# The last 512 output channels of a backbone layer's output projection kept in their own order, with a second copy of the router rows

## The chip, the cores and the metric

The kernel runs on one core of a Trainium2 chip. The metric is the device time of one execution in microseconds (us), as the median of several runs. Beside it stands one execution that the hardware profiler recorded; all durations below come from that execution. The engines are PE (TensorE; PEld is its weight load, the load of the stationary operand), DVE (VectorE), ACT (ScalarE), POOL (GpSimd) and SP, which here only issues DMAs.

## The reference, cut to what matters

One layer of a hybrid diffusion backbone, 256 latent and 256 context tokens, 2048 channels, float32:

```
mod  = silu(c) @ w_mod + b_mod                 # six vectors of 2048: sh1 sc1 g1 sh2 sc2 g2
u    = modulate(rmsnorm(h, norm_mix_w)) @ w_in
mix  = concat(ssd_branch(u), short_conv_branch(u)) @ w_out       # (4096) @ (4096, 2048)
h    = h + g1 * mix                                              # latent tokens only
f    = rmsnorm(h) * norm_ffn_w * (1 + sc2) + sh2
aff  = softmax(f @ w_router)                   # 16 experts; each takes its 32 best tokens
h    = h + g2 * expert_choice_ffn(f, aff, w_gate, w_up, w_down)
out  = rmsnorm(h)
```

The change lies in the output projection (`@ w_out`) for channels 1536 to 2047 and in the router product `f @ w_router` for the same channels.

## The kernel before

Large products run as three float32r passes: a weight tile is split into `whi` (rounded) and `wlo` (the rest), an activation likewise, and hi·hi, hi·lo and lo·hi are accumulated. `split_tile` does this for every tile of 128x1024 weights: SP loads `raw` (512 KB, L95, three buffers), ACT casts it to `whi` (L100), DVE subtracts to `wlo` (L101); `whi` and `wlo` also have three buffers. Its callers are the input projection (L338, `gemm_part`) and the output projection. Beside each tile run two paced streams: rows of `w_mod` for the second half of the modulation vectors (`mod_rows`: POOL loads a 256 KB `mraw`, DVE adds it to `macc`, L405, some 1.05 rows per tile in the output projection), and early loads of the first expert's weights into buffers as they come free (`first_weights`, L744, on SP's queue).

The output projection makes three passes over the 32 rows of 128 of `w_out`. Passes one and two (channels 0 to 1535, L856) hold the activations still and stream 512 weight columns. Pass three (channels 1536 to 2047, from `C3`) produces its result transposed: the weights are the stationary operand, 128 columns at a time, and 256 activations stream past. It takes 16 tiles; each needs 2 rows x 3 products x 4 column groups = 24 matmuls, 384 in all (L914). Which 128 of the 512 columns a group takes is what `in_fours` decides: group `i` takes columns `i, i+4, i+8, ...`, a step of four floats (16 bytes). The same order holds for the router: `w_router` lies in `gwr` as (block b, partition p, i), so its row `4p + i` of block b meets group `i`.

After pass three DVE adds the residual into `hT3` (tile `oh`, L918), ACT squares it (L920), PE accumulates the router's logits (L922) and the sums of squares (L925) into `pl`, and eight transposes bring `hT3` back into `h` (L930, copied by ACT at L931). From `pl` follow the softmax (L938 to L949), the choice of tokens (L967 on) and the gather of the first expert's tokens (L1038). Each expert then reads 24 MB of weights.

The order on each engine is set by a list scheduler from the order of the code; `issue_after` moves a block behind an instruction, `at_tick` delays it by so many weight tiles.

Of the kernel before, what the change touches and what calls it, by code (L numbers as in the profile page):

```python
# [11 lines left out]
OP = mybir.AluOpType  # L12
# [20 lines left out]
def layer(ctx: ExitStack, tc: tile.TileContext, x, c, cx, c_ctx, w_mod, b_mod, norm_mix_w, w_in,  # L33
# [27 lines left out]
    def sbank(name="s"):  # L61
        return bank("s", 4, name)
# [18 lines left out]
    def at_tick(n, fn):  # L81
        seq[0] += 1
        due.append((tick[0] + n, seq[0], fn))
# [48 lines left out]
    rows(r1[112:128], c_ctx)  # L132
    rows(r3, b_mod[0])

    r4 = pp.tile([13, 512], F32, name="r4")
    nc.gpsimd.dma_start(r4[0:4], norm_ffn_w[0].rearrange("(k p) -> k p", p=512))
    nc.gpsimd.dma_start(r4[4:12], b_mod[0, 3 * D:5 * D].rearrange("(k p) -> k p", p=512))
    nc.gpsimd.dma_start(r4[12:13], b_mod[0, 3 * D - 512:3 * D].rearrange("(k p) -> k p", p=512))
    hcol = const.tile([64, 2], F32, name="hcol")
    drow = pp.tile([2, KT], F32, name="drow")  # L140

# [65 lines left out]
    col2 = const.tile([P, 112], F32, name="col2")  # L207
    nc.vector.tensor_copy(col2, pt[:, 0:112])
    scw = col2[:, 0:48].rearrange("p (t k) -> p t k", t=3)
    nmix, _, nssm, nsc = (col2[:, 48 + 16 * i:64 + 16 * i] for i in range(4))  # L210

    pcol = const.tile([P, 3 * KT + 4], F32, name="pcol")
    nffn = pcol[:, 0:KT]

    cw = col1[:, 0:72].rearrange("p (t k) -> p t k", t=3)
# [3 lines left out]
    def late_cols():  # L219
        pt = sbank("pt")  # L220
        for i in range(4):
            nc.tensor.transpose(pt[:, 13 * i:13 * i + 13], r4.rearrange("p (c i) -> p i c", i=4)[:, i], ident[0:13, 0:13])
        nc.vector.tensor_copy(pcol.rearrange("p (a i) -> p i a", i=4),
                              pt[:, 0:52].rearrange("p (i c) -> p i c", i=4))
# [162 lines left out]

    mods = const.tile([P, 4, KT], F32, name="mods")
    sh2, G, g1c, g2c = (mods[:, i] for i in range(4))

    def mod_rows():

        for j in range(4):
            for q in range(4):
                dst = mods[:, j, 4 * q:4 * q + 4]
                c0 = (3, 4, 2, 5)[j] * D + 512 * q
                acc = mp.tile([P, 512], F32, name="macc", tag="macc", bufs=1)
                for k in range(KT):
# [9 lines left out]
                pc = sbank("pc")  # L408
                av = acc.rearrange("p (c i) -> p i c", i=4)
                fours = j < 2 or (j == 2 and q == 3)  # L410
                for i in range(4):
                    src = av[:, i] if fours else acc[:, P * i:P * i + P]
                    nc.tensor.transpose(pc[:, P * i:P * i + P], src, ident)

                def fin(j=j, q=q, dst=dst, c0=c0, pc=pc, fours=fours):
                    o = KT * (1 + j) + (4 * q if j < 2 else 0)
                    bias = pcol[:, o:o + 4] if fours else bcol[:, c0 // P:c0 // P + 4]
                    nc.vector.tensor_reduce(dst, pc.rearrange("p (j k) -> p j k", j=4), axis=mybir.AxisListType.X,
                                            op=OP.add)
                    nc.vector.tensor_tensor(dst, dst, bias, op=OP.add)  # L420
                    if j == 1:
                        nc.vector.scalar_tensor_tensor(dst, dst, 1.0, nffn[:, 4 * q:4 * q + 4], op0=OP.add, op1=OP.mult)
                at_tick(2, fin)
                yield

    def counted(steps):
# [366 lines left out]

    gwr = rp.tile([P, KT, 32], F32, name="gwr")
    wr = gwr[:, :, 0:NE]
    shw = hp_.tile([P, NE], F32, name="shw")
    g1 = []

    def prepare():
# [9 lines left out]
        nc.gpsimd.memset(gwr, 0.0)  # L809
        for b in range(4):  # L810
            nc.sync.dma_start(wr[:, 4 * b:4 * b + 4], w_router.rearrange("(b p i) e -> p b i e", p=P, i=4)[:, b])
        psb = sbank("psb")
        for k in range(KT):
            nc.tensor.matmul(psb[0:1, 0:NE], sh2[:, k:k + 1], wr[:, k], start=(k == 0), stop=(k == KT - 1))
# [8 lines left out]


    passes = ((0, 1024), (1024, 512))
    C3 = D - 512
# [59 lines left out]
    for i in range(0, 4, 2):  # L886
        pt = sbank("pt")
        for ii in range(2):
            for t in range(2):
                o = L * ii + P * t  # L890
                nc.tensor.transpose(pt[:, o:o + P], in_fours(h[:, t, C3:D])[:, i + ii], ident)
        nc.scalar.copy(hT3[:, i:i + 2], pt.rearrange("p (a b) -> p a b", a=2))

    pqs = rp.tile([P, L], F32, name="pqs", tag="hT", bufs=1)
# [12 lines left out]
    for k0 in range(0, 2 * KT, 2):  # L907
        hi, lo = split_tile(w_out, k0, C3, 512, 2)
        end = k0 == 2 * KT - 2
        todo = [(i, x) for x in products(k0, 2, hi, lo) for i in range(4)]  # L910
        if end:
            todo.sort(key=lambda x: x[0])
        for i, (j, pi, yy, w) in todo:
            nc.tensor.matmul(ov[i], in_fours(w[:, j])[:, i], yy, start=(k0 + j == 0 and pi == 0 and i % 2 == 0),  # L914
                             stop=(end and j == 1 and pi == 2), skip_group_check=True)
    for i in range(4):
        k = C3 // P + i
# [1 line left out]
        sq = rp.tile([P, L], F32, name="sq3", tag="hT" if i % 2 else "htmp", bufs=1)  # L919
        nc.scalar.activation(sq, hT3[:, i], AF.Square)  # L920
        for t in range(2):
            nc.tensor.matmul(pl[:, NE * t:NE * t + NE], hT3[:, i, P * t:P * t + P], gwr[:, k, 0:NE], start=False,  # L922
                             stop=(i == 3), skip_group_check=True)
        for t in range(2):
            nc.tensor.matmul(pl[:, 2 * NE + t:2 * NE + t + 1], sq[:, P * t:P * t + P], ones[:, 0:1], start=False,  # L925
                             stop=(i == 3), skip_group_check=True)
    for t in range(2):
        pt = sbank("pt")
        for i in range(4):
            nc.tensor.transpose(pt[:, P * i:P * i + P], hT3[:, i, P * t:P * t + P], ident)  # L930
        nc.scalar.copy(in_fours(h[:, t, C3:D]), pt.rearrange("p (i c) -> p i c", i=4))  # L931

    mod_rows_to(16 * KT)
    flush()
# [264 lines left out]
```

## Time and profile before

| | us |
|---|---|
| median of three runs (2007.34 to 2010.8) | 2009.35 |
| the profiled execution's own time | 2005.08 |
| its span in the trace | 2003.2 |
| output projection, passes one and two | 797 to 958 |
| output projection, pass three | 958 to 1052 |
| router, choice of tokens, gather | 1052 to 1078 |
| experts | 1078 to the end |

To read the profile: a stage is the stretch between two times of the trace; in it one looks for the engine that is never idle and for the wait that ends last. A PE pace is taken from the starts of its matmuls, not from their durations, since matmuls overlap.

### The profile page before, as it was taken

The page shows a single profiled execution, that of the slowest core. Times are in us where ns is not written, and L with a number is a line of the kernel's source. Part 1 is how long each engine was busy: PE and PEld are TensorE (multiplying, and loading weights), DVE is VectorE, ACT ScalarE, POOL GpSimd, SP SyncE. Part 2 cuts the span into 40 slices and gives each one's busy share as a digit, 9 for nine tenths or more (in the row PEclk, how much of TensorE's full clock was granted, in tenths as well). Part 3 has the DMA queues.
Part 4 walks back from the last instruction along what each step waited for, and adds up shares of the span by engine and source line. Part 5 has one row for each costly group of instructions (what it writes and reads, how often), then busy time and mean ns, then how long its engine had stood idle before and what let it go on. Part 6 is the DMA issues. An engine that isn't in the chain of part 4 may idle for free.

```text
span 2003.2 us, 25499 instructions
## 1 busy us (share of the span) xinstructions
PE 1671.1 (83%) x10340; PEld 1047.1 (52%) x10340; DVE 900.9 (45%) x1387; ACT 515.9 (26%) x847; POOL 183.9 (9%) x314
## 2 busy tenths in 40 slices
PE   6999999999999999999998766766766676666675
PEld 5677997878788999777993111111111111111122
DVE  2457985778778789777422111111011111101113
ACT  4323555574674344434211000000000000000002
POOL 1000110212112232322100000000000000000000
PEclk9999999999999999999998888888788888878888
DMA  9964783546367998888638999999999999999996
GB/s 356 405 230 121 238 266 101 164 125 216 89 209 257 341 301 298 293 315 291 214 128 327 422 428 427 427 427 428 426 428 427 428 426 427 427 428 427 427 427 259
DMA packets 149270, 641.12 MB, mean 320 GB/s; under 512 B 16649, under 2 KB 35334, under 8 KB 125216
## 3 DMA queue, kind: packets, MB, share of 16 engines
q1 hardware_dynamic: 127984, 570.19, 73.5%
q0 software_dynamic: 20880, 68.25, 9.9%
q8 instruction: 81, 1.33, 0.3%
q10 hardware_dynamic: 288, 1.05, 0.1%
q14 instruction: 37, 0.30, 0.0%
HBM read 637.34 MB, written 2.10 MB: 319 GB/s over the span
## 4 chain that ended last, share of the span: by engine, by line
DMA 44%; PE 39%; issue 7%; DVE 5%; ACT 2%; SPq 1%; POOL 1%; DVEq 0%; ACTq 0%; POOLq 0%
DMA abig<-in_w_up_dram 15%; PE g L335 11%; PE g L338 10%; DMA ebig<-in_w_up_dram 7%; DMA mwt<-in_w_up_dram 5%; DMA mwt<-in_w_down_dram 5%; PE gu L1076 4%; DMA mraw<-in_w_mod_dram 3%; DMA raw<-in_w_in_dram 3%; DMA ebig<-in_w_down_dram 3%; PE g L856 2%; DMA abig<-in_w_down_dram 2%; PE g L914 2%; PE yd L1109 2%; DVE wlo L101 2%
## 5 line engine op out<-in xcount | busy, mean ns | idle before, releaser
L338 PE MATMUL g<-abig,whi 128*128 128x256 f32 x2048 | 370.8, 285 | 4.9 <-ACT whi L100 2.8
L101 DVE TENSOR_TENSOR wlo<-raw,whi 128x1024 fp32r<-128x1024 f32 x241 | 295.7, 1230 | 168.2 <-ACT whi L100 167.0
L100 ACT CAST whi<-raw 128x1024 fp32r<-128x1024 f32 x241 | 254.0, 1055 | 381.9 <-DMA raw<-in_w_in_dram 87.2
L1076 PE MATMUL gu<-abig,xe 128*32 128x512 f32 x1200 | 247.0, 799 | 109.2 <-DMA abig<-in_w_up_dram 101.4
L338 PEld LDWEIGHTS g<-abig,whi 128*128 128x128 f32 x2048 | 316.8, 193 | 11.0 <-issue 5.4
L338 PE MATMUL g<-abig,wlo 128*128 128x256 f32 x1024 | 281.6, 286 | 1.7 <-DVE wlo L101 1.6
L1081 DVE SCALAR_TENSOR_TENSOR hid<-hid,gu 64x512 f32<-64x512 f32 x16 | 10.9, 679 | 496.4 <-ACT hid L1080 496.4
L335 PE MATMUL g<-abig,whi 128*128 128x512 f32 (+1 forms) x672 | 215.5, 399 | 3.7 <-ACT abig L319 2.0
L1076 PEld LDWEIGHTS gu<-abig,xe 128*32 128x32 f32 x1200 | 54.6, 139 | 274.6 <-DMA abig<-in_w_up_dram 133.7
L1080 ACT ACTIVATE hid<-gu 64x512 f32<-64x512 f32 x16 | 9.5, 591 | 729.1 <-PE gu L1076 729.1
L405 DVE SCALAR_TENSOR_TENSOR macc<-mraw,csl,macc 128x512 f32<-128x512 f32 x240 | 184.5, 769 | 26.4 <-DMA mraw<-in_w_mod_dram 23.8
L338 PEld LDWEIGHTS g<-abig,wlo 128*128 128x128 f32 x1024 | 192.8, 193 | 4.1 <-DVE wlo L101 3.2
L400 POOL DMA_DIRECT2D mraw<-in_w_mod_dram x256 | 138.2, 540 | 601.5 <-DVE macc L405 322.6
L1076 PE MATMUL gu<-ebig,xe 128*32 128x512 f32 x432 | 116.1, 812 | 53.7 <-DMA ebig<-in_w_up_dram 50.0
L1076 PE MATMUL gu<-mwt,xe 128*32 128x512 f32 x416 | 109.9, 791 | 41.4 <-DMA mwt<-in_w_up_dram 32.6
L335 PEld LDWEIGHTS g<-abig,whi 128*128 128x128 f32 (+1 forms) x672 | 122.4, 185 | 40.1 <-issue 8.8
L335 PE MATMUL g<-abig,wlo 128*128 128x512 f32 (+1 forms) x336 | 131.0, 394 | 0.0
L856 PE MATMUL g<-whi,abig 128*128 128x512 f32 x384 | 112.8, 397 | 4.7 <-ACT whi L100 4.6
L1123 DVE TENSOR_TENSOR m<-m,g 128x512 f32<-128x512 f32 x112 | 69.8, 682 | 62.9 <-PE g L1119 62.9
L1076 PEld LDWEIGHTS gu<-ebig,xe 128*32 128x32 f32 x432 | 24.2, 138 | 122.0 <-DMA ebig<-in_w_up_dram 64.3
L856 PEld LDWEIGHTS g<-whi,abig 128*128 128x128 f32 x384 | 72.4, 190 | 22.1 <-ACT whi L100 6.3
L1056 POOL DMA_DIRECT2D h<-in_final_norm_w_dram x1 | 0.6, 578 | 847.1 <-PE pt L1038 847.1
(339 smaller groups left out, 1855.4 us busy)
## 6 DMA issues: line engine op xcount, KB each, us to landing
raw<-in_w_in_dram SPq DMA_DIRECT2D x177, 512.0 KB, 4.6
abig<-in_w_gate_dram SPq DMA_DIRECT2D x35, 2048.0 KB, 38.7
abig<-in_w_up_dram SPq DMA_DIRECT2D x35, 2048.0 KB, 36.6
mraw<-in_w_mod_dram POOLq DMA_DIRECT2D x256, 256.0 KB, 4.5
abig<-in_w_down_dram SPq DMA_DIRECT2D x30, 2048.0 KB, 36.2
big<-in_w_mod_dram SPq DMA_DIRECT2D x32, 1024.0 KB, 10.8
raw<-in_w_out_dram SPq DMA_DIRECT2D x64, 512.0 KB, 5.2
mwt<-in_w_down_dram SPq DMA_DIRECT2D x16, 2048.0 KB, 34.8
```

Of the source, the lines that this page charges most:

```text
L100: nc.scalar.copy(hv, wv)
L101: sub = nc.vector.tensor_tensor(lv, wv, hv.bitcast(F32), op=OP.subtract)
L335: nc.tensor.matmul(banks[ct][0:ncol], st, a[q][:, kk], start=beg, stop=end)
L338: nc.tensor.matmul(banks[ct // 2][0:ncol, o:o + L], st, a[q][:, kk, L:2 * L], start=beg and ct % 2 == 0, stop=end, skip_group_check=True)
L400: nc.gpsimd.dma_start(w, w_mod[P * k:P * k + P, c0:c0 + 512])
L405: nc.vector.scalar_tensor_tensor(acc, w, cs, acc, op0=OP.mult, op1=OP.add)
L856: nc.tensor.matmul(ob[nn * t + m], yy[:, P * t:P * t + P], w[:, j, 512 * m:512 * m + 512], start=(k0 + j == order[0] and pi == 0), stop=(k ...
L914: nc.tensor.matmul(ov[i], in_fours(w[:, j])[:, i], yy, start=(k0 + j == 0 and pi == 0 and i % 2 == 0), stop=(end and j == 1 and pi == 2), ...
L1076: nc.tensor.matmul(gu[32 * q:32 * q + 32], xe[:, k], wt[q // 2][:, 1024 * kk + 512 * (q % 2):1024 * kk + 512 * (q % 2) + 512], start=(k == ...
L1081: nc.vector.scalar_tensor_tensor(hid, hid, 1.0, gu[0:64], op0=OP.add, op1=OP.mult)
L1109: nc.tensor.matmul(yd[32 * q:32 * q + 32], hidT[:, j, 32 * (c // 2):32 * (c // 2) + 32], parts[i][:, 512 * q:512 * q + 512], start=(c == 0 ...
L1123: nc.vector.tensor_tensor(av, h[:, t, 512 * q:512 * q + 512] if e_ == 0 else av, pc[q], op=OP.add)
```

## The change

The last 512 channels are no longer dealt out in fours. Each matmul of pass three takes 128 neighbouring columns as its stationary operand, and the two transposes of the residual ahead of it do the same. The router therefore needs its rows of these channels in their own order too: a tile `wr3` (128 x 4 x 16) is loaded a second time from `w_router`, in pieces of 16 floats, and multiplied by `G3`, a second copy of the factor norm_ffn_w * (1 + sc2) in that order. `G3` costs four more transposes and three small DVE instructions in `mod_rows` (one block of 512 columns is turned twice). The bias of `g1` for these channels comes from `bcol` now, so a 2 KB load at the start falls away. The eight transposes back into `h` are written behind the last sum of squares, and ACT's copy writes 512 neighbouring floats.

```diff
-    nc.gpsimd.dma_start(r4[12:13], b_mod[0, 3 * D - 512:3 * D].rearrange("(k p) -> k p", p=512))
...
+    G3 = const.tile([P, 4], F32, name="G3")
...
+                def columns(dst, fours, bias, norm):
+                    pc = sbank("pc")
+                    for i in range(4):
+                        src = av[:, i] if fours else acc[:, P * i:P * i + P]
+                        nc.tensor.transpose(pc[:, P * i:P * i + P], src, ident)
...
+                if j < 2:
+                    o = KT * (1 + j) + 4 * q
+                    columns(dst, True, pcol[:, o:o + 4], nffn[:, four] if j == 1 else None)
+                else:
+                    columns(dst, False, bias, None)
+                if j == 1 and q == 3:
+                    columns(G3, False, bias, nffn_[:, four])
...
+    wr3 = rp.tile([P, 4, NE], F32, name="wr3")
...
+        nc.sync.dma_start(wr3, w_router[C3:D].rearrange("(b p) e -> p b e", p=P))
+        nc.vector.tensor_tensor(wr3, wr3, G3.rearrange("p (k o) -> p k o", o=1).to_broadcast([P, 4, NE]), op=OP.mult)
...
-                nc.tensor.transpose(pt[:, o:o + P], in_fours(h[:, t, C3:D])[:, i + ii], ident)
+                nc.tensor.transpose(pt[:, o:o + P], h[:, t, C3 + P * (i + ii):C3 + P * (i + ii + 1)], ident)
...
-            nc.tensor.matmul(ov[i], in_fours(w[:, j])[:, i], yy, start=(k0 + j == 0 and pi == 0 and i % 2 == 0),
+            nc.tensor.matmul(ov[i], w[:, j, P * i:P * i + P], yy, start=(k0 + j == 0 and pi == 0 and i % 2 == 0),
...
-            nc.tensor.matmul(pl[:, NE * t:NE * t + NE], hT3[:, i, P * t:P * t + P], gwr[:, k, 0:NE], start=False,
+            nc.tensor.matmul(pl[:, NE * t:NE * t + NE], hT3[:, i, P * t:P * t + P], wr3[:, i], start=False,
...
-    for t in range(2):
-        pt = sbank("pt")
-        for i in range(4):
-            nc.tensor.transpose(pt[:, P * i:P * i + P], hT3[:, i, P * t:P * t + P], ident)
-        nc.scalar.copy(in_fours(h[:, t, C3:D]), pt.rearrange("p (i c) -> p i c", i=4))
+    with tc.issue_after(done.ins):
+        for t in range(2):
+            pt = sbank("pt")
+            for i in range(4):
+                nc.tensor.transpose(pt[:, P * i:P * i + P], hT3[:, i, P * t:P * t + P], ident)
+            nc.scalar.copy(h[:, t, C3:D], pt)
```

Within pass three the matmuls stand in the same order as before. At two places the instructions stand differently.

PE, before, at the end of pass three (L922 is the router's product, L925 the sums of squares, L930 the transposes back into `h`, L950 the turn of the softmax):

```order
L914 MATMUL g<-abig,whi 128x256
L922 MATMUL pl<-gwr,oh 128x16 x2
L930 MATMUL pt<-ident,oh 128x128 x4
L925 MATMUL pl<-ones,sq_10009 128x1 x2
L922 MATMUL pl<-gwr,oh 128x16 x2
L925 MATMUL pl<-ones,sq_10016 128x1 x2
L922 MATMUL pl<-gwr,oh 128x16 x2
L930 MATMUL pt<-ident,oh 128x128 x4
L925 MATMUL pl<-ones,sq_10023 128x1 x2
L922 MATMUL pl<-gwr,oh 128x16 x2
L925 MATMUL pl<-ones,sq_10030 128x1 x2
L950 MATMUL pa<-ident,aff 16x128 x2
```

PE, after, at the same place (the lines have moved by eleven or twelve):

```order
L925 MATMUL g<-abig,whi 128x256
L933 MATMUL pl<-wr_8224,oh 128x16 x2
L936 MATMUL pl<-ones,sq_10020 128x1 x2
L933 MATMUL pl<-wr_8224,oh 128x16 x2
L936 MATMUL pl<-ones,sq_10027 128x1 x2
L933 MATMUL pl<-wr_8224,oh 128x16 x2
L936 MATMUL pl<-ones,sq_10034 128x1 x2
L933 MATMUL pl<-wr_8224,oh 128x16 x2
L936 MATMUL pl<-ones,sq_10041 128x1 x2
L942 MATMUL pt<-ident,oh 128x128 x8
L962 MATMUL pa<-ident,aff 16x128 x2
```

The eight transposes stand behind the last sum of squares now, between it and the turn of the softmax.

SP, after, in pass one, where the router's rows are loaded (before, the three `gwr` loads stood behind twelve `raw` loads of `w_out`, with no `wr` load):

```order
L95 DMA raw<-in_w_out_dram 128x1024 x11
L822 DMA wr_8224<-in_w_router_dram 128x4x16
L95 DMA raw<-in_w_out_dram 128x1024
L821 DMA gwr<-in_w_router_dram 128x4x16 x3
L95 DMA raw<-in_w_out_dram 128x1024
```

The new load stands between the eleventh and the twelfth tile of `w_out`.

DVE, after, at the same place (the first `wlo` here is that of the ninth tile of `w_out`; `wr_8224` is `wr3`, `G_1528` is `G3`):

```order
L101 TENSOR_TENSOR wlo<-raw,whi 128x1024
L405 SCALAR_TENSOR_TENSOR macc<-mraw,csl,macc 128x512 x2
L101 TENSOR_TENSOR wlo<-raw,whi 128x1024
L823 TENSOR_TENSOR wr_8224<-wr_8224,G_1528 128x64
L101 TENSOR_TENSOR wlo<-raw,whi 128x1024
```

The product with `G3` stands between the tenth and the eleventh tile's subtraction; it is the first reader of the new load.

## Rows read from the trace of the kernel before

**Rows 1.** The page: PE's granted clock and the DMA engines' share, 40 slices.

```profile
PEclk9999999999999999999998888888788888878888
DMA  9964783546367998888638999999999999999996
```

**Rows 2.** Stretches: length, busy time (instructions) of PE, PEld, DVE, ACT, POOL; clock, DMA, GB/s.

```profile
690.00:740.00 50.00, 50.00 (x420) 50.00 (x419) 44.18 (x57) 22.00 (x25) 19.17 (x27) 1.00 0.90 298
740.00:790.00 50.00, 49.13 (x411) 48.93 (x410) 45.23 (x58) 23.03 (x27) 16.29 (x29) 1.00 0.96 326
850.00:900.00 50.00, 44.24 (x183) 34.51 (x184) 38.08 (x46) 17.14 (x19) 11.01 (x21) 0.97 0.89 318
957.80:1051.50 93.70, 93.70 (x416) 92.62 (x415) 29.46 (x38) 19.56 (x25) 4.31 (x8) 1.00 0.49 163
```

**Rows 3.** Groups in pass three: busy us, mean ns | idle before, releaser.

```profile
L101 DVE TENSOR_TENSOR wlo<-raw,whi 128x1024 fp32r<-128x1024 f32 x15 | 18.4, 1225 | 52.0 <-ACT whi L100 52.0
L100 ACT CAST whi<-raw 128x1024 fp32r<-128x1024 f32 x14 | 14.7, 1049 | 45.4 <-PE g L914 43.7 <-PE g L856 1.7
```

**Rows 4.** Lines L914 and L338: duration ns min/median/max; first and last start.

```profile
L914 PEld LDWEIGHTS g<-abig,whi x256: 307/330/334, 957.8 to 1051.6; 128*128 128x128 f32 x128
L338 PEld LDWEIGHTS g<-abig,whi x2048: 186/192/333, 199.5 to 799.9; 128*128 128x128 f32 x187
```

**Rows 5.** PE in order of time, in pass three and in the input projection.

```profile
997.41 2.03 PE L914 MATMUL g<-abig,whi 128*128 128x256 f32 x8
999.28 1.09 PE L914 MATMUL g<-abig,wlo 128*128 128x256 f32 x4
1000.21 2.03 PE L914 MATMUL g<-abig,whi 128*128 128x256 f32 x8
...
702.35 0.64 PE L338 MATMUL g<-abig,whi 128*128 128x256 f32 x4
702.83 0.28 PE L338 MATMUL g<-abig,wlo 128*128 128x256 f32 x1
```

**Rows 6.** Weight loads of line L413 in two blocks, columns in fours, then neighbouring.

```profile
L413 PEld LDWEIGHTS pc<-ident,macc x4: 198/204/210, 828.1 to 828.5; 128*128 128x128 f32 x4
...
L413 PEld LDWEIGHTS pc<-ident,macc x4: 138/140/142, 878.5 to 878.9; 128*128 128x128 f32 x4
```

**Rows 7.** All engines in order of time from pass three's end to the first expert.

```profile
1052.18 1.94 SPq L744 DMA_DIRECT2D abig<-in_w_gate_dram  x4
1052.35 0.63 PE L930 MATMUL pt<-ident,oh 128*128 128x128 f32 x4
1052.82 0.50 PE L925 MATMUL pl<-ones,sq 128*128 128x1 f32 x4
...
1054.52 0.63 PE L930 MATMUL pt<-ident,oh 128*128 128x128 f32 x4
...
1056.43 0.16 DVE L938 SCALAR_TENSOR_TENSOR rh<-pl,rh 128x2 f32<-128x2 f32 x1 [3.37 <-PE pl L925]
...
1071.71 3.81 PE L1038 MATMUL pt<-h,oh 128*32 128x512 f32 x16
...
1078.10 0.62 PE L1076 MATMUL gu<-ebig,xe 128*32 128x512 f32 x2 [1.18 <-DVE xe L1051]
```

**Rows 8.** DMA issues: KB each, median us from issue to landing.

```profile
raw<-in_w_out_dram SPq DMA_DIRECT2D x64, 512.0 KB, 5.2
ebig<-in_w_gate_dram SPq DMA_DIRECT2D x8, 512.0 KB, 9.2
gwr<-in_w_router_dram SPq DMA_DIRECT2D x4, 32.0 KB, 5.7
drow<-in_ssm_d_dram POOLq DMA_DIRECT2D x1, 0.1 KB, 7.2
```

**Rows 9.** DVE in pass one: subtractions of the eighth and the tenth tile of `w_out`.

```profile
819.04 1.23 DVE L101 TENSOR_TENSOR wlo<-raw,whi 128x1024 fp32r<-128x1024 f32 x1 [1.62 <-ACT whi L100]
...
825.07 1.21 DVE L101 TENSOR_TENSOR wlo<-raw,whi 128x1024 fp32r<-128x1024 f32 x1
```

More of the change, by code (lines that the diff above doesn't have):

```diff
@@ L133, in layer @@
     rows(r3, b_mod[0])
-    r4 = pp.tile([13, 512], F32, name="r4")
+    r4 = pp.tile([12, 512], F32, name="r4")
     nc.gpsimd.dma_start(r4[0:4], norm_ffn_w[0].rearrange("(k p) -> k p", p=512))
     nc.gpsimd.dma_start(r4[4:12], b_mod[0, 3 * D:5 * D].rearrange("(k p) -> k p", p=512))
-    nc.gpsimd.dma_start(r4[12:13], b_mod[0, 3 * D - 512:3 * D].rearrange("(k p) -> k p", p=512))
     hcol = const.tile([64, 2], F32, name="hcol")
@@ L209, in layer @@
     scw = col2[:, 0:48].rearrange("p (t k) -> p t k", t=3)
-    nmix, _, nssm, nsc = (col2[:, 48 + 16 * i:64 + 16 * i] for i in range(4))
-    pcol = const.tile([P, 3 * KT + 4], F32, name="pcol")
+    nmix, nffn_, nssm, nsc = (col2[:, 48 + 16 * i:64 + 16 * i] for i in range(4))
+    pcol = const.tile([P, 3 * KT], F32, name="pcol")
     nffn = pcol[:, 0:KT]
@@ L221, in late_cols @@
         for i in range(4):
-            nc.tensor.transpose(pt[:, 13 * i:13 * i + 13], r4.rearrange("p (c i) -> p i c", i=4)[:, i], ident[0:13, 0:13])
+            nc.tensor.transpose(pt[:, 12 * i:12 * i + 12], r4.rearrange("p (c i) -> p i c", i=4)[:, i], ident[0:12, 0:12])
         nc.vector.tensor_copy(pcol.rearrange("p (a i) -> p i a", i=4),
-                              pt[:, 0:52].rearrange("p (i c) -> p i c", i=4))
+                              pt[:, 0:48].rearrange("p (i c) -> p i c", i=4))
         nc.gpsimd.dma_start(hcol[:, 0:1], ssm_dt_bias.rearrange("o h -> h o"))
@@ L407, in mod_rows, with fin @@
                         yield
-                pc = sbank("pc")
                 av = acc.rearrange("p (c i) -> p i c", i=4)
-                fours = j < 2 or (j == 2 and q == 3)
-                for i in range(4):
[L412 to L423, printed above, removed]
+                def columns(dst, fours, bias, norm):
[3 more added lines that the diff above has]
+                        nc.tensor.transpose(pc[:, P * i:P * i + P], src, ident)
+                    def fin():
+                        nc.vector.tensor_reduce(dst, pc.rearrange("p (j k) -> p j k", j=4), axis=mybir.AxisListType.X,
+                                                op=OP.add)
+                        nc.vector.tensor_tensor(dst, dst, bias, op=OP.add)
+                        if norm is not None:
+                            nc.vector.scalar_tensor_tensor(dst, dst, 1.0, norm, op0=OP.add, op1=OP.mult)
+                    at_tick(2, fin)
+                four, bias = slice(4 * q, 4 * q + 4), bcol[:, c0 // P:c0 // P + 4]
+                if j < 2:
[5 more added lines that the diff above has]
+                    columns(G3, False, bias, nffn_[:, four])
                 yield
@@ L795, in layer @@
     wr = gwr[:, :, 0:NE]
+    C3 = D - 512
+    wr3 = rp.tile([P, 4, NE], F32, name="wr3")
     shw = hp_.tile([P, NE], F32, name="shw")
@@ L825, in layer @@
     passes = ((0, 1024), (1024, 512))
-    C3 = D - 512
     hs = const.tile([P, 2, 3], F32, name="hs")
@@ L921, in layer @@
         for t in range(2):
-            nc.tensor.matmul(pl[:, NE * t:NE * t + NE], hT3[:, i, P * t:P * t + P], gwr[:, k, 0:NE], start=False,
+            nc.tensor.matmul(pl[:, NE * t:NE * t + NE], hT3[:, i, P * t:P * t + P], wr3[:, i], start=False,
                              stop=(i == 3), skip_group_check=True)
         for t in range(2):
-            nc.tensor.matmul(pl[:, 2 * NE + t:2 * NE + t + 1], sq[:, P * t:P * t + P], ones[:, 0:1], start=False,
-                             stop=(i == 3), skip_group_check=True)
-    for t in range(2):
-        pt = sbank("pt")
-        for i in range(4):
-            nc.tensor.transpose(pt[:, P * i:P * i + P], hT3[:, i, P * t:P * t + P], ident)
-        nc.scalar.copy(in_fours(h[:, t, C3:D]), pt.rearrange("p (i c) -> p i c", i=4))
+            done = nc.tensor.matmul(pl[:, 2 * NE + t:2 * NE + t + 1], sq[:, P * t:P * t + P], ones[:, 0:1], start=False,
+                                    stop=(i == 3), skip_group_check=True)
+    with tc.issue_after(done.ins):
[4 more added lines that the diff above has]
+            nc.scalar.copy(h[:, t, C3:D], pt)
     mod_rows_to(16 * KT)
```

## The prediction, made before the changed kernel ran

> **What bounds the kernel now.** I read the slices first. The DMA engines are busy nine tenths or more from slice 22 on, that is through the experts, and there the granted clock is 0.8; slice 20, in pass three, has DMA at 3 tenths with the clock at 0.9 or more [rows 1]. So the experts are a DMA stage of fixed length, and whatever makes pass three end earlier moves them forward. Then the stretches: in pass three PE is busy 93.7 of 93.7 us at clock 1.00 (the 2.4 GHz level) while DMA stands at 0.49 and DVE and ACT at under a third [rows 2]. Next, who waits for whom there: ACT's cast waits 43.7 us for L914 to give back a `whi` buffer, and DVE waits 52.0 us for that cast [rows 3]. Nobody is late for PE. Pass three is a PE stage, and its pace is the question.
>
> The pace is odd. From 997.41 to 1000.21 PE starts 12 matmuls of L914, one each 233 ns; in the input projection four of L338 start in 0.48 us, one each 120 ns [rows 5]. Both have 128x128 float32r weights and 256 float32r activations as they stream, and the clock is 1.00 in both stretches [rows 2]. What differs in the operands is the step of the stationary one: neighbouring columns in L338, every fourth in L914. The weight load shows it: 330 ns in L914, 192 ns in L338 [rows 4]. A second pair settles most of the doubt: line L413 turns blocks of `macc` with the columns taken in fours for some blocks and in a row for others, and the same instruction loads its weights in 204 ns in the first case and in 140 ns in the second [rows 6].
>
> **The change part by part.** The sum goes from the profiled execution's own time, 2005.08 us (span 2003.2), which lies 4.3 us under the median of the runs, 2009.35; I take the same difference off the median.
>
> *Pass three's matmuls.* 384 matmuls go from 233 to 120 ns: 384 x 0.1133 = **43.5 us off** the path. The step is the same in all 384, the tile shape is that of L338, so I take L338's pace whole. Pass three would last some 93.7 - 43.5 = 50.2 us.
>
> *What is late next in pass three.* At the new pace a tile takes 2.88 us, as in the input projection, whose loads have the same size and whose `mod_rows` stream is no slower. There PE kept busy 50.00 and 49.13 of 50 us at 298 and 326 GB/s [rows 2]. Pass three moves 93.7 us x 163 GB/s = 15.3 MB; in 50.2 us that is 304 GB/s, between those two. The worst stretch at such a load is 850 to 900, where early loads stood between the `raw` loads: 44.24 of 50 busy at 318 GB/s [rows 2]. So the bounds are 0 and 12% of 50 = 6 us; I take 3%, **1.5 us on**, near the two stretches with the same matmuls, since in pass three the `raw` loads run ahead of most early loads. DMA time is no harder bound: 0.49 x 93.7 = 46 us of it fits in 50, at a share of 0.91, and 0.96 was reached [rows 2].
>
> *The end of pass three.* Four transposes stand between products and sums of squares twice. The next L925 starts 0.47 us after each L930 group begins [rows 7], and the second sum of squares frees the buffer that the next square needs. With both groups behind the last L925, DVE's L938 comes about 2 x 0.47 = **1 us** sooner. The transposes then fill the time in which PE waits for the softmax; the gather that reads `h` starts 15 us after L938 [rows 7], so they and ACT's copies cost nothing (without that cover some 2 us). Bounds 0 to 2.
>
> *The second copy.* G3 adds four transposes in the input projection, where PE is the bound: four at 0.12 us or a little more, **0.5 us on**. Its three DVE instructions lie in a stage where DVE is busy 44 to 45 of 50 us [rows 2]: about 1 us fits in the gaps; uncovered it would be that 1 us. The 2 KB load that goes, the contiguous transposes of the residual and the contiguous copy into `h` lie beside other work: nothing.
>
> *The load of `wr3`.* It is a wait in DVE's queue that was not there. SP issues it behind the eleventh `raw`, whose buffer is free when the eighth subtraction ends, at 820.3; DVE reaches the product behind the tenth, at 826.3 [rows 9]. That is 6.0 us of cover. Queued behind it on DVE stand the eleventh `wlo` and all `macc` work, and PE waits for that `wlo`; on SP the twelfth `raw` waits for the ninth subtraction anyway. The router's other loads, 128 pieces of 256 bytes each, land in 5.7 us; 32 pieces of 4 bytes (`drow`) in 7.2; half a megabyte queued among others in 9.2 [rows 8]. `wr3` has 512 pieces of 64 bytes, which no row shows. Near the first three the wait is 0 to 3.2 us, and PE has about a tile's subtraction of lead, 1.2 us. I take **1 us on**, bounds 0 and 3; the far bound is a rival below.
>
> Sum: -43.5 + 1.5 - 1.0 + 0.5 + 1.0 = -41.5 us. The profiled execution would take 1963.6 us, the median 2009.35 - 41.5 = 1967.9, so **1968 us**.
>
> *Behind pass three* nothing should give the gain back. The last four early loads start when pass three frees its last buffer, at 1052.18, and the first expert's matmuls at 1078.10, after the chain through the softmax [rows 7]. Both ends of that 26 us stretch hang on the end of pass three, so it moves as a piece, and the experts behind it read the same bytes.
>
> **The rivals.**
>
> *DMA becomes the bound of pass three* (the ring of three `raw` buffers runs dry). For it: pass three would ask 304 GB/s where it now asks 163, and in its second half half-megabyte early loads stand between the `raw` loads; such loads have taken 9.2 us to land [rows 8]. A buffer's round is landing, cast (1.05) and subtraction (1.23) [rows 3]: at 9.2 us, 11.5 / 3 = 3.8 us for a tile, 0.95 over the 2.88, for some 8 tiles 7.6 us; with the bound of 6 us for the rest of the pass 14 us at most. Against it: at 5.2 us [rows 8] a round gives 2.5 us for a tile, and buffers are ahead at the start, as ACT's waits show [rows 3]. It would give 1974 to 1982 us.
>
> *No gain in the pace.* L914 also goes round four accumulators, one matmul each, where L338 stays on one, and that might set 233 ns. Against it: the weight load itself is longer, and L413 differs by the step alone [rows 4, 6]. Then only the small terms are left, 0.5 + 1 - 1 us (without the faster pace nothing is late in pass three), about 2010 us. The Trainium skill has a rule that would come to this: "TensorE: Matmul & The Clock Gate", section "LDWEIGHTS (loading the stationary operand)", gives the time of a weight load as the number of columns over 1.2, 107 ns for 128, with nothing on their step. The trace disagrees with it by 330 against 192 ns at the same 128 columns, so it gets little of the chance.
>
> *Slower: the `wr3` load stalls DVE.* Place: DVE's queue between the tenth and the eleventh subtraction, 826.3. If time went by pieces, at `drow`'s 7.2 / 32 = 0.225 us each, 512 pieces would take 115 us; less 6 of cover and 1 of lead, 108 us on, and 2009 - 42.5 + 108 = 2075 us. It makes the kernel slower from a landing of about 7 + 42 = 50 us. Against it: 128 pieces land in 5.7 us, less than `drow`'s 32 [rows 8], so most of the 7.2 us is no time for pieces.
>
> **How the numbers follow.** Forecast 0.81, DMA-bound pass three 0.13, no gain 0.04, slower 0.02. The forecast's own range: the terms at their low ends give -43.5 - 2 + 0.5 = -45 us, 1964, less 2 to 4 us for the spread of the runs and for the lower profiled execution, 1960; at the high ends -43.5 + 6 + 0.5 + 3 = -34 us, 1975. To take in the greater part of the second case the range goes to 1979. Faster than before by over 0.2% (4 us, about what a measurement of this kernel can tell from no change): 0.81 + 0.13 = 0.94; within 0.2%: 0.04; slower: 0.02.
>
> **What would show it.** In the profile after: weight loads of pass three at about 192 ns and a start each 120 ns; pass three some 50 us long with PE busy over 95% and DMA at about 0.9; the first expert's matmuls some 42 us earlier; the experts' length unchanged; the first L936 straight behind the router's product; DVE's product for `wr3` with a wait of under 3 us in front. The prediction is wrong if the loads stay at 330 ns; if they fall but PE idles over 6 us in pass three; or if pass three ends 42 us earlier and the first expert doesn't.

## The result and the profile after

The changed kernel takes 1965.04 us, the median of four runs (1960.28 to 1965.16), against 2009.47 for four runs of the kernel before (2007.34 to 2010.8): a ratio of 0.9774, 95% interval 0.9757 to 0.9791, so 44.4 us less. The forecast was 1968, range 1960 to 1979. The profiled execution of after took 1965.03 us (span 1963.2), that of before 2005.08 (span 2003.2). Those two differ by 40.05 us, and the stages below are compared between them.

| stage | before | after | difference |
|---|---|---|---|
| start of the trace to pass three's first matmul | 958.01 | 958.65 | +0.64 |
| pass three, first matmul to first router product | 93.98 | 50.22 | -43.76 |
| first router product to first expert's first matmul | 26.11 | 26.70 | +0.59 |
| first expert's first matmul to the end of the span | 925.1 | 927.6 | +2.5 |
| sum (span) | 2003.2 | 1963.2 | -40.0 |

The page of after, granted clock and DMA share in 40 slices of 49 us (counted from 0, as in the prediction), answers to [rows 1]:

```profile
PEclk9999999999999999999989877878888889888787
DMA  9964784455465999899898999999999999999996
```

The dip to 3 tenths in slice 20 is gone: pass three now lies in slices 19 and 20, at 8 and 9 tenths. The stretches of pass three and of the time before it (length; busy time and instructions of PE, PEld, DVE, ACT, POOL; clock, DMA share, GB/s) answer to [rows 2]:

```profile
850.00:900.00 50.00, 46.26 (x201) 36.10 (x197) 39.37 (x48) 17.81 (x19) 11.82 (x22) 0.93 0.92 325
958.60:1008.90 50.30, 50.30 (x419) 49.17 (x418) 29.17 (x37) 18.97 (x25) 4.30 (x8) 1.00 0.85 302
```

Pass three is still a PE stage. PE is busy 50.30 of 50.30 us at clock 1.00 (the 2.4 GHz level), and DMA went from 0.49 to 0.85, 163 to 302 GB/s. The matmul line of pass three, now L925 (duration ns min/median/max, first and last start), and its pace in order of time answer to [rows 4] and [rows 5]:

```profile
L925 PEld LDWEIGHTS g<-abig,whi x256: 186/192/201, 958.4 to 1008.6; 128*128 128x128 f32 x128
...
L925 PE MATMUL g<-abig,whi x256: 278/283/384, 958.6 to 1008.8; 128*128 128x256 f32 x128
```

```profile
986.37 1.12 PE L925 MATMUL g<-abig,whi 128*128 128x256 f32 x8
987.33 0.64 PE L925 MATMUL g<-abig,wlo 128*128 128x256 f32 x4
```

A weight load takes 192 ns instead of 330. Eight matmuls start in 987.33 - 986.37 = 0.96 us, one each 120 ns. ACT's group in pass three (busy us, mean ns | idle before, releaser) answers to [rows 3]:

```profile
L100 ACT CAST whi<-raw 128x1024 fp32r<-128x1024 f32 x14 | 14.7, 1049 | 20.2 <-DMA raw<-in_w_out_dram 13.3 <-PE g L925 5.3 <-PE g L867 1.7
```

ACT used to wait 43.7 us for PE to give buffers back; now it waits 13.3 us for a `raw` tile to land and 5.3 us for PE. The supply has come near the demand, yet none of that wait reaches PE.

### The profile page after: what moved, and what is told of

It reads as the page before. It is cut to its first block, busy times and chain, and to the rows that moved or that the text cites. A ratio compares the mean times of both kernels' runs of the same rounds, so it can differ in the third digit from the quotient of the medians.

```text
span 1963.2 us, 25512 instructions
## 1 busy us (share of the span) xinstructions
PE 1640.9 (84%) x10344; PEld 1007.1 (51%) x10344; DVE 901.1 (46%) x1391; ACT 515.5 (26%) x847; POOL 185.6 (9%) x313
## 3 DMA queue, kind: packets, MB, share of 16 engines
q8 instruction: 81, 1.33, 0.3%
## 4 chain that ended last, share of the span: by engine, by line
PE 44%; DMA 42%; DVE 7%; issue 3%; ACT 2%; SPq 1%; POOL 0%; ACTq 0%; DVEq 0%; POOLq 0%
DMA abig<-in_w_up_dram 14%; PE g L334 11%; PE g L337 10%; DMA ebig<-in_w_up_dram 9%; DMA mwt<-in_w_up_dram 5%; DMA mwt<-in_w_down_dram 5%; PE gu L1088 5%; PE g L867 3%; PE yd L1121 3%; PE g L925 2%; DMA mraw<-in_w_mod_dram 2%; DMA raw<-in_w_in_dram 2%; DVE wlo L101 2%; DMA ebig<-in_w_down_dram 2%; DMA raw<-in_w_out_dram 2%
## 5 line engine op out<-in xcount | busy, mean ns | idle before, releaser
L1088 PE MATMUL gu<-abig,xe 128*32 128x512 f32 x1200 | 242.0, 774 | 111.1 <-DMA abig<-in_w_up_dram 97.1
L1088 PE MATMUL gu<-mwt,xe 128*32 128x512 f32 x416 | 116.8, 832 | 42.7 <-DMA mwt<-in_w_up_dram 32.5
```

Of the source, the lines that this page charges most:

```text
L1088: nc.tensor.matmul(gu[32 * q:32 * q + 32], xe[:, k], wt[q // 2][:, 1024 * kk + 512 * (q % 2):1024 * kk + 512 * (q % 2) + 512], start=(k == ...
```

## The experiments

Theory: the step of four floats in the stationary operand sets the pace of pass three, by itself, and the other parts of the change are worth about a microsecond together. Rivals: the rotation round four accumulators sets the pace; the other parts hide a gain or a loss; or a step costs in the weight load alone. Trace rows are of pass three where nothing else is said; its length there is from the first weight load to the start of the last matmul (94.0 us before, 50.4 after).

**The step alone, in the kernel before.**

```diff
-            nc.tensor.matmul(ov[i], in_fours(w[:, j])[:, i], yy, ...
+            nc.tensor.matmul(ov[i], w[:, j, P * i:P * i + P], yy, ...
```

> The kernel before with one edit: the matmuls of pass three take 128 neighbouring columns as their stationary operand; the router rows, the residual and the way back stay dealt out in fours (so the last 512 channels are summed in mixed order; the amount of work is the same). Theory (the step of the stationary operand sets the pace): weight loads of pass three 192 ns instead of 330, a matmul each 120 ns instead of 233, pass three about 50 us, the time about 1966 us, the whole gain of the change within 3 us. Rival (part of the gain comes from the other edits: router copy, moved transposes, contiguous copies): it stays over 1972 us.

Measured: 1967.31 us (1964.68 to 1968.18) against 2007.34 on the same chip, ratio 0.9797, interval 0.9768 to 0.9827: 40.0 us less. The weight load line of this kernel:

```profile
L914 PEld LDWEIGHTS g<-abig,whi x256: 186/192/203, 961.0 to 1011.4; 128*128 128x128 f32 x128
```

One edited line takes the loads to 192 ns and pass three to 50.5 us. The accumulators rotate as before, so they don't set the pace. Of the 44.4 us of the whole change the step alone gives 40.0, though its pass three is as short as that of after.

**The step put back, in the kernel after.**

```diff
-            nc.tensor.matmul(ov[i], w[:, j, P * i:P * i + P], yy, ...
+            nc.tensor.matmul(ov[i], in_fours(w[:, j])[:, i], yy, ...
```

> The changed kernel with that one edit undone: pass three takes every fourth column again, all else as changed (mixed order of the last 512 channels, same work). Theory: pass three back at 94 us, the time at 2008 to 2012 us; the rest of the change costs or gives under 3 us. Rival (the other edits carry some of the gain): under 2004 us.

Measured: 2004.69 us (ten runs, 2002.33 to 2008.16) against the same 2007.34, ratio 0.9986, interval 0.9973 to 0.9999.

```profile
L925 PEld LDWEIGHTS g<-abig,whi x256: 307/330/334, 955.9 to 1049.6; 128*128 128x128 f32 x128
L925 PE MATMUL g<-abig,whi x256: 282/395/508, 956.1 to 1049.8; 128*128 128x256 f32 x128
```

The loads are back at 330 ns, the matmuls last 395 instead of 283, and pass three is at 93.9 us. So the rest of the change (second copy, contiguous transposes and residual, moved transposes) takes 2.8 us off, 0.2 to 5.4 by the interval, where I expected a small cost. The moved transposes' 0.8 us is part of it; where more of it lies is said below, with the rest of the change.

**Other steps.** Three kernels change only which columns a stationary operand takes: steps of two, three and eight.

```diff
+ step 2:  w[:, j, 256 * (i // 2):256 * (i // 2) + 256].rearrange("p (c i) -> p i c", i=2)[:, i % 2]
+ step 3:  w[:, j, i:i + 384].rearrange("p (c i) -> p i c", i=3)[:, 0]
+ step 8:  w.rearrange("p a b -> p (a b)").rearrange("p (c i) -> p i c", i=8)[:, 4 * j + i]
```

> The changed kernel with a step of two in the stationary operand of pass three (8 bytes; columns in mixed order, same work). If the cost grows with the bytes stepped over, the weight load lies about a third of the way from 192 to 330 ns, near 240, and pass three between 55 and 70 us. If only neighbours are cheap and any step costs the same: 330 ns and 94 us. If the price begins at 16 bytes: 192 ns and 50 us.

> The changed kernel with a step of three floats (12 bytes) in the stationary operand of pass three (some columns taken twice, some not at all; same work). The step of two cost nothing (195 ns), that of four all of it (330 ns). If the price begins only at four floats: 195 ns, pass three 50 us. If it grows from two to four: near 260 ns, pass three 60 to 75 us.

> The changed kernel with a step of eight floats (32 bytes) in the stationary operand (columns of both rows of the tile, mixed order, same work). If the price is one for every step from four floats on: 330 ns and 94 us, as with four. If it grows with the bytes: over 500 ns, pass three over 150 us.

The same line in the three kernels, step 2, then 3, then 8 (one fence each):

```profile
L925 PEld LDWEIGHTS g<-abig,whi x256: 193/195/209, 956.3 to 1006.7; 128*128 128x128 f32 x128
```

```profile
L925 PEld LDWEIGHTS g<-abig,whi x256: 250/263/269, 953.6 to 1025.6; 128*128 128x128 f32 x128
```

```profile
L925 PEld LDWEIGHTS g<-abig,whi x256: 312/337/344, 954.5 to 1051.1; 128*128 128x128 f32 x128
```

With the lengths of pass three, the pace is 120 ns plus what the length has over 50.4 us, divided by 384:

| step (bytes) | weight load, ns | pass three, us | ns per matmul | time of the kernel |
|---|---|---|---|---|
| 1 (4), after | 192 | 50.4 | 120 | 1965.04 |
| 2 (8) | 195 | 50.5 | 120 | 1962.65, a single run |
| 3 (12) | 263 | 72.1 | 177 | 1977.56, a single run |
| 4 (16), put back | 330 | 93.9 | 233 | 2004.69 |
| 8 (32) | 337 | 96.7 | 241 | 2008.25, a single run |

A step of two is free, three costs half, four the whole, and eight hardly more than four. At steps of one, two, three and four or more, four, two, on average 1.33 and one of the elements read lie in the same 16 bytes. From a step of two on the load grows with the new 16 bytes that an element needs (0.5, 0.75, 1 and 1 for 195, 263, 330 and 337 ns); from one to two, 0.25 to 0.5, it stays at 192 to 195. That is a reading of five times, not a test of the memory. The Trainium skill, "SBUF — State Buffer", section "Door 1: The DMA port swizzle (why `[64,N]` ≈ `[32,N]`)", says that lines are 16 bytes and that two hits in a line are wanted for full speed: the runs agree, step 2 being free at 195 ns. It goes on that four fp32 can be stepped for free; there the measurement differs, 330 ns at step four.

**The step on the streaming operand.** The weights stay contiguous, and the 256 activations are taken at a step of four.

```diff
...
-                yield j, pi, yy[i][:, kk], w
+                mv = yy[i][:, kk]
+                if fours:
+                    g = kk // 4 * 4
+                    mv = yy[i][:, g:g + 4].rearrange("p a l -> p (a l)").rearrange("p (c i) -> p i c", i=4)[:, kk % 4]
+                yield j, pi, mv, w
...
```

> The changed kernel with the streaming operand of pass three taken with a step of four instead (256 activations, every fourth of 1024; tokens and rows in mixed order, same work), the stationary one contiguous. If any operand of a matmul with such a step costs as the stationary one did: the pace at 200 ns or more and pass three over 80 us. If the price belongs to the weight load alone: a matmul each 120 ns, pass three 50 us, 1965 us.

Measured: 2009.95 us in a single run.

```profile
L929 PEld LDWEIGHTS g<-abig,whi x256: 186/208/209, 960.7 to 1054.1; 128*128 128x128 f32 x128
L929 PE MATMUL g<-abig,whi x256: 394/418/477, 960.9 to 1054.3; 128*128 128x256 f32 x128
```

Now the weight load is near that of after (208 against 192 ns) and the matmul is the long one, 418 against 283 ns. Pass three takes 93.6 us, a matmul each 120 + (93.6 - 50.4) / 0.384 = 232 ns. The price of a step of four is the same on either operand here, though 128 columns are loaded and 256 streamed.

**The eight transposes in their old place.** The kernel after, with the `issue_after` block undone.

```diff
-    with tc.issue_after(done.ins):
-        for t in range(2):
-            pt = sbank("pt")
...
+    for t in range(2):
+        pt = sbank("pt")
```

> The changed kernel with the eight transposes back into h written where they stood before (between the router's products and the sums of squares). If they cost what the prediction took, the step that follows the last sum of squares (the sum's first reader on DVE) comes 0.8 to 1.0 us later after the last matmul of pass three than in the changed kernel (3.7 us there, 4.6 before the change): 4.5 us or more. If the scheduler moves them out of the way by itself or the squares bound the chain: 3.7 us.

Measured: 1965.34 us in a single run. The chain behind the first router product in this kernel, then in after (start, us, engine, line, operation, idle before and its releaser):

```profile
1008.55 0.51 PE L933 MATMUL pl<-wr,oh 128*128 128x16 f32 x4
...
1013.00 0.16 DVE L949 SCALAR_TENSOR_TENSOR rh<-pl,rh 128x2 f32<-128x2 f32 x1 [3.37 <-PE pl L936]
```

```profile
1008.87 0.51 PE L933 MATMUL pl<-wr,oh 128*128 128x16 f32 x4
...
1012.36 1.07 PE L942 MATMUL pt<-ident,oh 128*128 128x128 f32 x8
1012.53 0.16 DVE L950 SCALAR_TENSOR_TENSOR rh<-pl,rh 128x2 f32<-128x2 f32 x1 [2.59 <-PE pl L936]
...
1020.82 5.52 PE L973 MATMUL warm<-g2r,ident 128*128 128x512 f32 x8 [0.67 <-ACT g2r L969]
...
1035.57 0.62 PE L1088 MATMUL gu<-ebig,xe 128*32 128x512 f32 x2 [1.18 <-DVE xe L1063]
```

From the first L933 to `rh` it is 4.45 us with the transposes in the old place and 3.66 in the new: 0.8 us for the move, which the trace shows and the total can't. (The last two rows, the idle matmuls and the first expert's start, answer to the end of [rows 7].)

**No idle matmuls ahead of the choice of tokens.** Both kernels run four matmuls into `warm` (eight in the trace) while DVE chooses tokens; PE then has the next products in its queue behind them.

```diff
-WARM = 4
+WARM = 0
```

> The changed kernel without the four idle matmuls behind the choice of tokens (their result is read by nobody; the output is the same). The matmul that spreads the chosen tokens stands behind them on PE and its input is ready some 3 us before they end. If that wait is on the chain to the first expert: from the last choice step to the gather about 8.5 us instead of 11.6 to 13.4, and up to 3 us off the time, unless the clock falls in the gap: then the gather's 16 matmuls and the first expert's run at the lower level and take it back. Either way the four idle matmuls are what made the changed kernel's profile lose 1.8 us there (5.5 us for them instead of 3.7).

Measured: 1958.18 us (1954.93 to 1961.6), ratio 0.9760, interval 0.9741 to 0.9778. On the same chip the kernel after was timed again, as a base for this run and for the next but one:

> The changed kernel itself, timed again beside the next one on the same chip. The first timing gave 1965.0 us (1960.3 to 1965.2). If the terms of the sum are right and the rest is where the clock falls in the tail, it lies between 1960 and 1967 us again.

It gave 1962.83 us (1960.56 to 1964.4), ratio 0.9778, interval 0.9762 to 0.9794, and its pass three repeats the first trace of after:

```profile
956.40:1006.70 50.30, 50.30 (x418) 49.17 (x417) 29.24 (x37) 18.90 (x25) 4.29 (x8) 1.00 0.85 303
```

So the median without the idle matmuls is 4.6 us lower. The two intervals overlap (0.9762 to 0.9778), but three of its four runs lie under every run of after. The end of the choice and the gather, first of the repeat, then of the kernel without them:

```profile
1017.92 0.42 DVE L979 MAX8 gi<-nxt 16x8 f32<-16x256 f32 x1
1018.29 3.70 PE L973 MATMUL warm<-g2r,ident 128*128 128x512 f32 x8 [0.68 <-ACT g2r L969]
...
1021.92 0.48 PE L996 MATMUL pi__10124<-bd,ones 16*128 16x128 f32 x2
...
1024.86 3.79 PE L1050 MATMUL pt<-h,oh 128*32 128x512 f32 x16
```

```profile
1016.48 0.42 DVE L979 MAX8 gi<-nxt 16x8 f32<-16x256 f32 x1
...
1018.09 0.45 PE L996 MATMUL pi__10120<-bd,ones 16*128 16x128 f32 x2 [1.80 <-DVE bd L993]
...
1021.41 3.81 PE L1050 MATMUL pt<-h,oh 128*32 128x512 f32 x16
```

The first product of the chosen tokens, L996, follows the last choice by 4.00 us with the idle matmuls in front of it and by 1.61 without, and the gather starts 4.9 us after that choice instead of 6.9. Without them the granted clock in the gather is 0.50, the lower level (1.2 GHz), where the repeat has 1.00, the upper one, and yet the gather takes 3.81 us against 3.79. The gather's stretch, of the repeat, then without them:

```profile
1024.80:1028.60 3.80, 3.80 (x19) 0.51 (x18) 0.77 (x3) 0.00 (x0) 0.35 (x1) 1.00 0.99 412
```

```profile
1021.40:1025.20 3.80, 3.80 (x18) 0.60 (x17) 0.61 (x2) 0.00 (x0) 0.00 (x0) 0.50 0.97 410
```

From the first router product to the first expert's matmul it is 24.5 us in the repeat and 22.4 without them: 2.1 of the 4.6 us lie there in the traces. Another 2.6 lie in the experts, 927.8 and 925.2 us, and are not traced to the idle matmuls (see the experts' length below).

**The last expert's end.** In the first trace of after the last expert's final groups ran longer than in that of before. Three idle matmuls were put ahead of each of its last three weight groups, to keep the clock up.

```diff
...
+            if e_ == NE - 1 and k0 >= 4:
+                for _ in range(TAIL):
+                    nc.tensor.matmul(warm2, ident, g2r, start=True, stop=True)
```

> The changed kernel with three idle matmuls of 512 columns ahead of each of the last three groups of weight tiles of the last expert, in gaps where PE waits for its weights (their result is read by nobody; the output is the same). In the changed kernel's profile the last expert's matmuls ran partly at the lower level of the clock, 3 us more than before the change. If the clock falls because PE idles between the tiles: the clock at 1.00 in the last 35 us, and the end 2 to 3 us sooner, about 1962 us, with less spread. If the falls come at times of their own: no difference, 1965 us, or up to 2 us more where the idle matmuls stand in the way.

Measured: 1961.19 us (1960.09 to 1962.31), ratio 0.9774, interval 0.9758 to 0.979. That settles nothing: the scheduler put the idle matmuls ahead of the gaps that they were meant to fill (16 of the trace's 18 start from 1891.14 on and two at 1901.78, while the three long waits end at 1909.44, 1914.35 and 1919.28), and the clock fell to 0.66 there all the same:

```profile
1915.00:1925.00 10.00, 6.12 (x28) 1.36 (x28) 0.00 (x0) 0.00 (x0) 0.00 (x0) 0.66 1.03 389
```

**The gather without its step.** If the streaming operand pays for a step of four, so does the gather, which takes `h` in fours. Here it streams `h` in a row, and the four turns behind it take the fours instead.

```diff
-                                     in_fours(h[:, t, 512 * q:512 * q + 512]), ...
+                                     h[:, t, 512 * q:512 * q + 512], ...
...
-                nc.tensor.transpose(pt[:, P * j:P * j + P], xg[:, P * j:P * j + P], ident)
+                nc.tensor.transpose(pt[:, P * j:P * j + P], in_fours(xg)[:, j], ident)
```

> The changed kernel with the same idea at another operand: the gather of an expert's tokens streams 512 neighbouring channels instead of every fourth, and the turn behind it takes the columns in fours as its stationary operand instead (the result is the same). From the run with the streaming operand at a step of four (pace 233 ns instead of 120): the 16 matmuls of the first expert's gather, 3.8 us on the chain from the router to the first expert, fall to about 2 us, and the four turns grow by under 0.2 us. If the experts move with that chain, 1.5 to 2 us off, about 1963 us; if the gather is bound by something else (it runs four row groups side by side), 3.8 us stays and the time is that of the changed kernel.

> The gather with neighbouring channels (as in e9_gather), on the same chip as the changed kernel. Its chain from pass three to the first expert was 1.8 us shorter in the gather. If that reaches the end: 1 to 2.5 us under the changed kernel's median. If the spread of the tail hides it: within 1 us of it.

Measured: 1962.38 us (1960.1 to 1965.35), ratio 0.9784, interval 0.9768 to 0.9801; again, beside the repeat of after: 1960.32 us (1956.26 to 1967.28), ratio 0.9765, interval 0.9741 to 0.9789. The gather's line in after, then here:

```profile
L1050 PE MATMUL pt<-h,oh x256: 1058/1080/1130, 1029.2 to 1877.5; 128*32 128x512 f32 x128
```

```profile
L1050 PE MATMUL pt<-h,oh x256: 592/592/1061, 1024.5 to 1871.1; 128*32 128x512 f32 x128
```

A matmul goes from 1080 to 592 ns, and the first expert's matmuls start 4.6 us after the gather begins instead of 6.4. Against the repeat of after that is 2.5 us less in the median, but the intervals overlap, so the total can't confirm the 1.8 us. The clock may take some of it back: in both traces of this kernel it stood at 0.65 in the first expert's first 5 us, in both of after at 1.00, and from there to the end of the span it is 929.1 us in both, against 927.6 and 927.8. That the gather brings it is not shown: with the old gather it stood at 0.64 to 0.65 there in three other kernels (the step alone, steps of two and of eight). The first trace of this kernel, then the repeat of after:

```profile
1029.10:1034.00 4.90, 4.88 (x32) 1.42 (x36) 0.30 (x1) 0.00 (x0) 0.00 (x0) 0.65 0.03 12
```

```profile
1031.20:1036.00 4.80, 4.77 (x48) 1.48 (x52) 0.31 (x1) 0.00 (x0) 0.00 (x0) 1.00 0.10 14
```

## Why the prediction was right, point by point

The forecast of 1968 us missed the median by 3 us, and the time lies inside the range. Its main mechanism was shown, by the step alone and by its undoing; of the small terms one came out as forecast, two were too large, and one stays open.

- **Pass three's matmuls, -43.5.** Right. Pass three is 43.76 us shorter from first matmul to first router product, at 120 ns a matmul and 192 ns a weight load. L338's pace [rows 4, 5] was the right row to lean on. L413's pair [rows 6] showed less than I took from it: its loads differ by 64 ns, but its pace hardly does (last section).
- **Stalls in pass three, +1.5 (0 to 6).** Too much: 0. DMA moved 302 GB/s (304 forecast), and the casts wait 13.3 us for landings, but PE never idles. The row of 850 to 900 was a far one; the two stretches of the input projection, with the same matmuls, were the ones to take whole. The rival of a DMA-bound pass falls with it.
- **The end of pass three, -1.0 (0 to 2).** Right to a fifth: 0.8 us from the first product to `rh`, and the old place gives it back.
- **The load of `wr3`, +1.0 (0 to 3).** Too much: 0. In after SP issues it, DVE ends its tenth subtraction and reads it:

```profile
823.45 0.43 SPq L822 DMA_DIRECT2D wr<-in_w_router_dram  x1
...
828.02 1.22 DVE L101 TENSOR_TENSOR wlo<-raw,whi 128x1024 fp32r<-128x1024 f32 x1
829.15 0.22 DVE L823 TENSOR_TENSOR wr<-wr,G 128x64 f32<-128x64 f32 x1
...
DMA to landing us min/median/max: 4.9/4.9/4.9
```

The landing took 4.9 us and the product starts 829.15 - 823.88 = 5.3 us after the issue ends, with no idle time in front of it. The cover was 0.7 us less than worked out, and the price nearer the bottom of its bounds: 512 pieces of 64 bytes were no slower than 128 of 256 [rows 8]. The slower rival (108 us of stall) is far off.

- **The second copy, +0.5.** Not resolved. Over all profiles of this study passes one and two start between 797.4 and 802.9 us with or without `G3`.
- **The rest of the change together.** I had +0.5 -1.0 +1.0, that is +0.5 us, without the faster pace; the undone step gives -2.8 (-5.4 to -0.2). Wrong in sign. The `wr3` term's 1 us was the over-sized part that a row shows; without it the sum is -0.5. A place for the remainder stands in the traces, though not its cause: passes one and two, whose stalls I had not taken to fall. From their first matmul to pass three's first they last 160.6 us in before and 159.6 with the step alone, and 154.7 to 159.0 in the twelve profiles that have the rest of the change (in the pair of the table a start 2.8 us later hides it). PE waits there for ACT's `whi` 4.6 and 3.0 us in the first two, 0 to 2.1 in the twelve; in before, then in after:

```profile
L856 PE MATMUL g<-whi,abig 128*128 128x512 f32 x384 | 112.8, 397 | 4.7 <-ACT whi L100 4.6
```

```profile
L867 PE MATMUL g<-whi,abig 128*128 128x512 f32 x384 | 112.4, 397 | 0.9 <-ACT whi L100 0.9
```

The router's loads and DVE's new instructions stand in that stretch; which part of the change shortens it no run separates, and two traces on one side are few.

- **"The experts' length unchanged".** In this pair of traces it is 2.5 us longer. The last expert's final groups, in before, in after, and in the repeat of after:

```profile
1965.71 4.96 PE L1076 MATMUL gu<-abig,xe 128*32 128x512 f32 x28 [3.39 <-DMA abig<-in_w_up_dram]
...
1973.84 1.93 PE L1139 MATMUL yd<-mwt,hidT 128*32 128x256 f32 x32 [0.52 <-ACT hidT L1091]
...
1970.00:1975.00 5.00, 2.26 (x32) 1.05 (x32) 1.39 (x3) 0.96 (x2) 0.00 (x0) 1.00 1.05 387
```

```profile
1923.23 6.50 PE L1088 MATMUL gu<-abig,xe 128*32 128x512 f32 x28 [3.55 <-DMA abig<-in_w_up_dram]
...
1932.90 3.38 PE L1151 MATMUL yd<-mwt,hidT 128*32 128x256 f32 x32 [0.52 <-ACT hidT L1103]
...
1932.00:1937.00 5.00, 4.48 (x40) 2.31 (x40) 0.91 (x3) 0.37 (x1) 0.00 (x0) 0.66 0.92 330
```

```profile
1919.20 6.38 PE L1088 MATMUL gu<-abig,xe 128*32 128x512 f32 x28 [3.68 <-DMA abig<-in_w_up_dram]
...
1928.74 3.32 PE L1151 MATMUL yd<-mwt,hidT 128*32 128x256 f32 x32 [0.52 <-ACT hidT L1103]
```

The two groups are 1.5 and 1.45 us longer in after, with the clock at 0.66 where it was 1.00: 3.0 us. The repeat has them nearly as long, and its experts last 927.8 us, so in both traces of the changed kernel this part of the forecast did not hold. Whether the change brings it is not shown. Over all profiles of this study it is 925.1 to 929.2 us from the first expert's matmul to the end of the span. With a slow pass three it is short in three (before, step put back, step of three: 925.1 to 925.3) and long in two (step of eight 929.2, streaming step 927.4); with the fast one it is long in eight of nine and short without the idle matmuls (925.2). So the pace of pass three alone does not decide it. Two stretches at a low clock make up the spread, the one in the last expert and the one in the first expert's first 5 us. Where the latter has 0.64 or 0.65 (five profiles) it is 889.1 to 889.5 us from the first expert's matmul to the last expert's final `gu` group; where it has 1.00 (nine) it is 887.6 to 888.0. The chain ahead of the experts has the same kind of difference between two executions of one kernel: its idle matmuls took 5.52 us in the first trace of after and 3.70 in the repeat, as in before; these 1.8 us are more than the 0.8 won by the move.

That the total came so close is partly luck. By the stages of the table the forecast was +1.5, -42.0, -1.0 and 0, and the two traces gave +0.64, -43.76, +0.59 and +2.5: errors of both signs, which leave -41.5 against -40.05. Against the medians, 44.4 us apart, the forecast is 2.9 us short.

The "no gain" rival (the accumulators) falls by the step alone. The trace of before had already held a row against it that I did not use: its last tile stays on one accumulator for several matmuls, and runs at the slow pace nonetheless (the three starts take 0.70 us):

```profile
1047.55 0.40 PE L914 MATMUL g<-abig,wlo 128*128 128x256 f32 x1
...
1048.25 0.40 PE L914 MATMUL g<-abig,wlo 128*128 128x256 f32 x1
```

## What to carry to other kernels

Look at how far apart the elements of a matmul's operands lie, the streaming one too: where a PE stage runs at half the pace of a like stage at the same clock, compare the weight load's and the matmul's durations of both. The matmul was longer with either operand at a step of four (395 and 418 ns against 283); the weight load was long only when the step was in its own operand (330 ns; 208 with the step on the streaming side). A layout that deals channels out in fours cost each matmul of pass three that read it in fours 113 ns; a second small copy was nearly free here, and a step of two on the stationary operand cost nothing in the one kernel that had it. Of work that was put on an engine to keep its clock up, ask what waits behind it: the kernel without the four idle matmuls was the fastest of this study.

## What the runs showed that I had not expected

- The price of a step grows in between, 195, 263, 330, 337 ns at 2, 3, 4 and 8 floats, and is about the same 113 ns a matmul at step four on a streamed operand of twice the columns.
- Transposes hardly feel it. The residual's transposes (L891 before, L902 after) had weight loads of 213 ns and now have 140, in before and then in after:

```profile
L891 PEld LDWEIGHTS pt<-ident,h x8: 199/213/223, 966.7 to 973.6; 128*128 128x128 f32 x8
```

```profile
L902 PEld LDWEIGHTS pt<-ident,h x8: 138/140/158, 963.2 to 967.1; 128*128 128x128 f32 x8
```

Yet from the first of four to the matmul behind the fourth it is 0.40 us before and 0.35 after, so that a step costs a transpose some 12 ns of its pace and a pass-three matmul 113. The two blocks of L413 in [rows 6] are nearly alike from the first start to the last end, in fours and then in a row:

```profile
828.29 0.63 PE L413 MATMUL pc<-ident,macc 128*128 128x128 f32 x4
...
878.70 0.60 PE L413 MATMUL pc<-ident,macc 128*128 128x128 f32 x4
```

A longer weight load alone did not tell the pace there.

- The gather, which streams at a step of four, takes the same time at either level of the clock: 3.81 us at 0.50 and 3.79 at 1.00. So the clock that the idle matmuls kept up gave nothing there, while they held the chain up: 1962.83 with them, 1958.18 without.
- Three kernels of the study that were run several times lie under the changed one (1962.83 and 1965.04) in their medians: the one without the idle matmuls (1958.18), the one with the contiguous gather (1960.32 and 1962.38) and the one with idle matmuls at the last expert (1961.19). The first two edits together were not run.
